# Output projection with weight rows outermost, 512 columns in four PSUM banks, for four of six token groups

## The chip, the cores and the metric

The kernel runs on one core of one Trainium2 chip. The metric is the device time of one execution in microseconds (us), lower is better. The engines work from queues of their own: TensorE (PE in the rows; PEld is its weight load), VectorE (DVE), ScalarE (ACT), GpSimd (POOL) and SyncE (SP, which here only issues DMAs). They meet through semaphores.

## The reference, cut to what matters

Two token groups, p (1024 tokens) and s (512 tokens), go through the same two layers. Each layer projects the normed input, runs three attention or convolution branches of 1280 columns together, gates them, and ends with the step that is changed here:

```python
y = jnp.concatenate([y1, y2, ym], axis=-1)          # (tokens, 1280)
x = x + (y * jax.nn.silu(z)) @ w_out[l]             # w_out[l]: (1280, 1024)
```

Layer 0 feeds layer 1, whose first step is an RMS norm over the rows of x.

## The kernel before

**Output projection.** `out_proj` handles 512 tokens at a time, so there are six token groups: p layer 0 halves 0 and 1, s layer 0, p layer 1 halves 0 and 1, s layer 1. Every fp32 operand is split into a high and a low part, and each product is three matmuls: high by high, high by low, low by high (L322, L323, L324 in `mm_a`). The outer loop takes 256 of the 1024 output columns at a time (`ci`, four of them). For each, `load_w` fetches five weight tiles of 256 KB (two rows of 128 contraction channels by 256 columns) and splits them. Then come four tiles of 128 tokens, and inside each the ten contraction rows k: 4 x 4 x 10 x 3 = 480 matmuls of 256 columns per group. Two token tiles share one PSUM bank of tag "d" (two banks in all); when both are complete, VectorE adds the residual at L935 and the sum goes to DRAM, as 8 evictions and 8 stores per group.

**Buffers.** `whi`, `wlo` (split weights) have 7 buffers, `wraw` 3, `bw` (residual rows among others) 5, `act` (gated branch outputs `ahi`, `alo`) 16. PSUM has two banks each of tags s, t and d, and one each of x and o. The banks of tag "t" hold the transposed probabilities `pT`, the small sums `ss` and the gate rows `rbT` of attention.

**Order of the work.** `STEPS` lists the phases. A planner then orders each engine's queue at compile time from this list and its own estimate of times. Attention phases (`ax`, `diff`, `mem_attn`) are marked urgent, so projections fill TensorE in between. `in_order` adds one more rule: the tiles of one ring (tag and stream) are first written in the order of the list. On the chip each queue runs in the order that was laid down.

**Around the groups.** Each layer 0 group of p is followed by a norm (`norm_steps`): load rows of x1, square, scale, transpose on TensorE (`hT`), store. It is doled out by `between` in the matmul loops. The list ends with attention of s layer 1, "diff s 2", "diff s 3", "mem s 1", and then the three last output projections: p layer 1 half 0, p layer 1 half 1, s layer 1. The last needs the results of "mem s 1" (`ym`).

Of the kernel before, what the change touches and what calls it, by code (L numbers as in the profile page):

```python
# [9 lines left out]
F32 = mybir.dt.float32  # L10
BF16 = mybir.dt.bfloat16
F32R = mybir.dt.float32r
ACTF = mybir.ActivationFunctionType
ALU = mybir.AluOpType
# [23 lines left out]
STEPS = [  # L38
# [11 lines left out]
]  # L50
BUF_TABLE = {
# [30 lines left out]
def trunk_kernel(ctx: ExitStack, tc: tile.TileContext, a: dict, dbg=None):  # L82
    nc = tc.nc
# [93 lines left out]
    S = {}  # L177
# [36 lines left out]
        return g  # L214

    @first
    def load_w(src, pairs):
        hi, lo = [], []
        for kp in pairs:
            lo_ = ring(sb, [128, 2, 256], F32R, "wlo", "wlo")  # L220
            h = ring(sb, [128, 2, 256], F32R, "whi", "whi")
            raw = ring(sb, [128, 2, 256], F32, "wraw", "wraw")
            dma(out=raw, in_=src[kp].rearrange("p (k n) -> p k n", k=2))
            split(h, lo_, raw, nc.vector if kp % 2 == 0 else nc.gpsimd)
            hi.append(h)
            lo.append(lo_)
        return hi, lo

    def rstd(out, ss, mul, add):
# [84 lines left out]
    def mm_a(out, hs, sl, w, mid=None):  # L314

        whi, wlo = w
        n = 2 * len(hs)
        for k in range(n):
            hi, lo = hs[k // 2]
            h, l_ = hi[:, k % 2, sl], lo[:, k % 2, sl]  # L320
            wh, wl = whi[k // 2][:, k % 2, :], wlo[k // 2][:, k % 2, :]
            nc.tensor.matmul(out=out, lhsT=h, rhs=wh, start=(k == 0), stop=False)  # L322
            nc.tensor.matmul(out=out, lhsT=h, rhs=wl, start=False, stop=False)  # L323
            nc.tensor.matmul(out=out, lhsT=l_, rhs=wh, start=False, stop=(k == n - 1))  # L324
            if mid and k == n // 4:
                mid()

    def mm_b(out, hs, w, csl, mid=None):

        whi, wlo = w  # L330
        n = 2 * len(hs)
        for k in range(n):
            hi, lo = hs[k // 2]
            h, l_ = hi[:, k % 2, :], lo[:, k % 2, :]
            wh, wl = whi[k // 2][:, k % 2, csl], wlo[k // 2][:, k % 2, csl]
            nc.tensor.matmul(out=out, lhsT=wh, rhs=h, start=(k == 0), stop=False)  # L336
            nc.tensor.matmul(out=out, lhsT=wh, rhs=l_, start=False, stop=False)  # L337
            nc.tensor.matmul(out=out, lhsT=wl, rhs=h, start=False, stop=(k == n - 1))  # L338
            if mid and k == n // 4:
                mid()  # L340
# [577 lines left out]
    def out_proj(g, l, hf, ys, ahead=None):  # L918
        T = GROUPS[g]
        src = a[f"x_{g}"] if l == 0 else S[g, "x1"]  # L920
        dst = S[g, "x1"] if l == 0 else a[f"out_{g}"]
        for ci in range(4):
            if ahead and ci == 3:
                ahead()
            w = load_w(a["w_out"][l, ci], Y_ORDER[g, l])
            for tp in range(2):
                ps = ring(psum, [128, 2, 256], F32, "d", "po")
                for t in range(2):
                    tt = 2 * tp + t
                    mm_a(ps[:, t, :], ys, slice(tt * 128, (tt + 1) * 128), w, lambda: between(0))  # L930
                rows = slice(hf * 512 + tp * 256, hf * 512 + (tp + 1) * 256)
                cols = slice(ci * 256, (ci + 1) * 256)
                xr = bw("xr").rearrange("p (t n) -> p t n", t=2)
                dma(out=xr, in_=src[rows, cols].rearrange("(t p) n -> p t n", p=128))
                nc.vector.tensor_tensor(out=xr, in0=ps, in1=xr, op=ALU.add)  # L935
                dma(out=dst[rows, cols].rearrange("(t p) n -> p t n", p=128), in_=xr)


    nxt = {}
# [27 lines left out]
    YS, YM = {}, {}  # L967
# [6 lines left out]
    def step(op, g, *x):  # L974
        if op == "in":
            l = int(x[0])
# [32 lines left out]
        elif op == "loady":  # L1009
            settle()  # L1010
            l, hf = int(x[0]), int(x[1])
            part = slice(int(x[2]), int(x[3])) if len(x) > 2 else slice(0, 5)
            YS.setdefault((g, l, hf), []).extend(load_y(g, l, hf, part))
        elif op == "memkv":
            mem_kv(1, H["m"])
        elif op == "out":
            l, hf = int(x[0]), int(x[1])
            out_proj(g, l, hf, YS[g, l, hf] + ([YM[l]] if g == "s" else []))
        elif op == "settle":
            settle()  # L1020

# [9 lines left out]
def host_arrays(inputs):  # L1031
# [29 lines left out]
    def pieces(w, idx):  # L1061
# [8 lines left out]
    out["mem_s"] = f["mem_sample"][0]  # L1070
    out["w_in"] = np.stack([np.stack([pieces(f["w_in"][l], cols(l, *c)) for c in CHUNKS[l]]) for l in range(2)])
    out["w_out"] = np.stack(
        [np.stack([pieces(f["w_out"][l], np.arange(256 * c, 256 * c + 256)) for c in range(4)]) for l in range(2)])
    out["w_mem_kv"] = np.stack(
        [np.stack([pieces(f["w_mem_kv"][l], np.arange(256 * c, 256 * c + 256)) for c in range(2)]) for l in range(2)])
    out["conv_w"] = f["conv_w"][0].reshape(3, 4, 128).transpose(2, 1, 0)
# [58 lines left out]
```

## Time and profile before

| | us |
|---|---|
| median of 3 runs | 2108.88 (2107.57 to 2109.26) |
| the profiled execution | 2099.39 |
| span of the profiled execution | 2097.6 |
| TensorE busy | 2040.2 |
| VectorE busy | 1552.4 |
| ScalarE busy | 1115.9 |
| GpSimd busy | 969.9 |

Busy times are unions of an engine's instructions. Matmuls overlap in the pipeline, so the time from one start to the next, not a matmul's own duration, is what one costs.

### The profile page before, as it was taken

What the parts mean: (1) busy time and instruction counts of PE and PEld (TensorE: products, weight loads), DVE (VectorE), ACT (ScalarE), POOL (GpSimd) and SP (SyncE); (2) the same over time, 40 slices, a digit from 0 to 9 for tenths busy, and PEclk for the clock granted to TensorE, in tenths of its full rate; (3) what the DMA queues carried; (4) which work ended last, traced back from release to release, by engine and by line L of the source; (5) the groups of instructions that cost most, each with busy time, mean ns of one, the idle gap of its engine ahead of it and who ended that gap; (6) DMA issues with size and microseconds to landing.
All of it is one profiled execution on the core that took longest, in us unless ns stands there. A gap on an engine that the chain in (4) does not pass through costs nothing.

```text
span 2097.6 us, 40483 instructions
## 1 busy us (share of the span) xinstructions
PE 2040.2 (97%) x14056; PEld 1885.0 (90%) x14056; DVE 1552.4 (74%) x3340; ACT 1115.9 (53%) x2634; POOL 969.9 (46%) x994
## 2 busy tenths in 40 slices
PE   6999999999999999999999899999998999999999
PEld 6999888889999899998999888888997898989999
DVE  8779877645446697887869998878879877876642
ACT  5545433453334466665667655566566665654531
POOL 6753422342224564645636564343363785833411
PEclk9999999999999999999999999999999999999999
DMA  7786733336777732354255756466576567577753
GB/s 236 206 241 197 228 106 91 118 101 217 238 236 224 209 93 82 104 154 128 82 151 154 226 164 178 151 199 213 169 218 199 160 191 193 157 235 225 233 159 106
DMA packets 323420, 365.79 MB, mean 174 GB/s; under 512 B 28048, under 2 KB 229520, under 8 KB 323216
## 3 DMA queue, kind: packets, MB, share of 16 engines
q1 hardware_dynamic: 323216, 363.21, 58.1%
q8 instruction: 111, 1.82, 0.4%
q14 instruction: 93, 0.76, 0.1%
HBM read 263.48 MB, written 99.61 MB: 173 GB/s over the span
## 4 chain that ended last, share of the span: by engine, by line
PE 75%; DMA 7%; DVE 7%; issue 3%; POOL 2%; ACT 1%; SPq 1%; DVEq 0%; POOLq 0%; ACTq 0%
PE pb L338 8%; PE pb L336 8%; PE pb L337 8%; PE pa L323 5%; PE pa L324 5%; PE pa L322 5%; PE po L322 4%; PE po L323 4%; PE po L324 4%; PE s L596 4%; PE s L597 4%; PE o L754 3%; PE pT L750 3%; PE o L685 1%; PE pT L683 1%
## 5 line engine op out<-in xcount | busy, mean ns | idle before, releaser
L200 POOL TENSOR_TENSOR wlo<-wraw,whi 128x512 fp32r<-128x512 f32 x182 | 249.0, 1370 | 329.1 <-ACT whi L199 309.9
L695 ACT ACTIVATE e<-s,nm 128x512 f32<-128x512 f32 (+1 forms) x416 | 265.1, 640 | 221.2 <-DVE nm L693 167.4
L199 ACT CAST whi<-wraw 128x512 fp32r<-128x512 f32 x388 | 236.9, 622 | 238.8 <-PE po L324 84.6
L604 DVE TENSOR_TENSOR ptlo<-pT,pthi 128x512 fp32r<-128x512 f32 x352 | 237.3, 683 | 41.6 <-ACT pthi L603 40.0
L693 DVE TENSOR_REDUCE nm<-s 128x1 f32<-128x512 f32 (+1 forms) x368 | 249.0, 682 | 25.7 <-PE s L597 24.4
L603 ACT CAST pthi<-pT 128x512 fp32r<-128x512 f32 x352 | 199.1, 588 | 114.6 <-PE pT L683 56.6
L322 PE MATMUL po<-whi,ahi 128*128 128x256 f32 x896 | 254.0, 284 | 0.4 <-DVE xr L935 0.4
L324 PE MATMUL po<-whi,alo 128*128 128x256 f32 x896 | 253.1, 284 | 1.3 <-DVE alo L200 1.3
L323 PE MATMUL po<-wlo,ahi 128*128 128x256 f32 x896 | 254.2, 284 | 0.0
L200 DVE TENSOR_TENSOR wlo<-wraw,whi 128x512 fp32r<-128x512 f32 x206 | 170.8, 830 | 95.3 <-ACT whi L199 92.5
L236 POOL TENSOR_TENSOR rs<-ss,mhalf 128x8 f32<-128x8 f32 (+2 forms) x108 | 141.1, 1307 | 174.4 <-DVE ss L232 125.2
L322 PE MATMUL pa<-whi,ahi 128*128 128x256 f32 x768 | 220.2, 287 | 0.5 <-ACT raw L394 0.4
L324 PE MATMUL pa<-whi,alo 128*128 128x256 f32 x768 | 219.2, 286 | 0.5 <-DVE alo L200 0.5
L323 PE MATMUL pa<-wlo,ahi 128*128 128x256 f32 x768 | 219.2, 285 | 0.0
L596 PE MATMUL s<-k,qhh 128*128 128x512 f32 (+2 forms) x512 | 190.1, 376 | 10.5 <-ACT e L695 9.6
L597 PE MATMUL s<-k,qll 128*128 128x512 f32 (+2 forms) x512 | 182.9, 363 | 2.8 <-DMA qll<-st_p1mq 1.6
L324 PEld LDWEIGHTS po<-whi,alo 128*128 128x128 f32 x896 | 171.0, 191 | 3.2 <-DVE alo L200 1.7
L322 PEld LDWEIGHTS po<-whi,ahi 128*128 128x128 f32 x896 | 171.1, 191 | 1.9 <-DVE xr L935 0.6
L323 PEld LDWEIGHTS po<-wlo,ahi 128*128 128x128 f32 x896 | 171.1, 191 | 1.2
L336 PE MATMUL pb<-h,whi 128*128 128x512 f32 x432 | 170.9, 396 | 0.0
L338 PE MATMUL pb<-h,wlo 128*128 128x512 f32 x432 | 170.7, 395 | 0.0
L337 PE MATMUL pb<-h,whi 128*128 128x512 f32 x432 | 170.6, 395 | 0.0
(170 smaller groups left out, 6022.7 us busy)
## 6 DMA issues: line engine op xcount, KB each, us to landing
wraw<-in_w_in_dram SPq DMA_DIRECT2D x252, 256.0 KB, 3.3
wraw<-in_w_out_dram SPq DMA_DIRECT2D x120, 256.0 KB, 3.2
alo<-y_p SPq DMA_DIRECT2D x20, 512.0 KB, 5.3
zg_p<-z SPq DMA_DIRECT2D x32, 256.0 KB, 2.7
v<-dv_p SPq DMA_DIRECT2D x16, 512.0 KB, 5.5
k<-st_p1dk SPq DMA_DIRECT2D x16, 512.0 KB, 4.3
zg<-zg_p SPq DMA_DIRECT2D x48, 128.0 KB, 3.0
y_p<-yo SPq DMA_DIRECT2D x48, 128.0 KB, 2.4
```

The source lines that it names most:

```text
L200: lo_eng.tensor_tensor(out=out_lo, in0=src, in1=f32(out_hi), op=ALU.subtract)
L322: nc.tensor.matmul(out=out, lhsT=h, rhs=wh, start=(k == 0), stop=False)
L323: nc.tensor.matmul(out=out, lhsT=h, rhs=wl, start=False, stop=False)
L324: nc.tensor.matmul(out=out, lhsT=l_, rhs=wh, start=False, stop=(k == n - 1))
L336: nc.tensor.matmul(out=out, lhsT=wh, rhs=h, start=(k == 0), stop=False)
L337: nc.tensor.matmul(out=out, lhsT=wh, rhs=l_, start=False, stop=False)
L338: nc.tensor.matmul(out=out, lhsT=wl, rhs=h, start=False, stop=(k == n - 1))
L596: nc.tensor.matmul(out=out, lhsT=q2[0], rhs=k, start=True, stop=False)
L597: nc.tensor.matmul(out=out, lhsT=q2[1], rhs=k, start=False, stop=True)
L604: nc.vector.tensor_tensor(out=lo, in0=ps, in1=f32(hi), op=ALU.subtract)
L693: nc.vector.tensor_reduce(out=nm, in_=s, axis=AXL.X, op=ALU.max, negate=True)
L695: nc.scalar.activation(out=e[:, j, :], in_=s[:, j, :], func=ACTF.Exp, bias=nm[:, j:j + 1], accum_out=su[:, j:j + 1],)
```

## The change

Four of the six groups (both halves of p layer 0, half 1 of p layer 1, s layer 1) use a new function, `out_proj_k`. It takes 512 columns at a time, with the weight rows k as the outer loop and four token tiles inside, each in a PSUM bank of its own: two of tag "d" and two of tag "t". That is 2 x 10 x 4 x 3 = 240 matmuls of 512 columns per group. The weights in DRAM are laid out anew (before the launch) as rows of 512 columns; the two groups that keep `out_proj` read their 256 columns out of these rows in pieces of 1 KB. The list of phases keeps its order.

```diff
-    "loady p 0 1", "out p 0 0", "norm p 0", "out p 0 1", "norm p 1", "load m", "load p 1 01", "memkv m",
+    "loady p 0 1", "outk p 0 0", "norm p 0", "outk p 0 1", "norm p 1", "load m", "load p 1 01", "memkv m",
...
-    "loady p 1 1", "out p 1 0", "loady s 1 0 0 4", "out p 1 1", "out s 1 0",
+    "loady p 1 1", "out p 1 0", "loady s 1 0 0 4", "outk p 1 1", "outk s 1 0",
...
-    def load_w(src, pairs):
+    def load_w(src, ks, wide=False):
+        for k in ks:
...
+            raw = ring(sb, [128, 512], F32, "wraw", "wraw")
+            dma(out=raw if len(src.shape) == 3 else raw.rearrange("p (i n) -> p i n", i=2), in_=src[k])
+            split(h, l_, raw, nc.vector if k % 2 == 0 else nc.gpsimd)
...
-            w = load_w(a["w_out"][l, ci], Y_ORDER[g, l])
+            w = load_w(
+                a["w_out"][l, ci // 2][:, :, ci % 2 * 256:ci % 2 * 256 + 256].rearrange("(k i) p n -> k p i n", i=2), Y_ORDER[g, l]
+            )
...
+    def out_proj_k(g, l, hf, ys):
+        src = a[f"x_{g}"] if l == 0 else S[g, "x1"]
+        dst = S[g, "x1"] if l == 0 else a[f"out_{g}"]
+        order = [2 * kp + i for kp in Y_ORDER[g, l] for i in range(2)]
+        for ci in range(2):
+            cols = slice(ci * 512, (ci + 1) * 512)
+            rows = [slice(hf * 512 + t * 128, hf * 512 + (t + 1) * 128) for t in range(4)]
+            ps = [ring(psum, [128, 512], F32, "d", "pk") for _ in range(2)]
+            ps += [ring(psum, [128, 512], F32, "t", "pk", "A") for _ in range(2)]
+            xr = []
+            for n, k in enumerate(order):
+                (wh,), (wl,) = load_w(a["w_out"][l, ci], [k], True)
+                hi, lo = ys[n // 2]
+                for t in range(4):
+                    sl = slice(t * 128, (t + 1) * 128)
+                    h, l_ = hi[:, n % 2, sl], lo[:, n % 2, sl]
+                    nc.tensor.matmul(out=ps[t], lhsT=h, rhs=wh, start=(n == 0), stop=False)
+                    nc.tensor.matmul(out=ps[t], lhsT=h, rhs=wl, start=False, stop=False)
+                    nc.tensor.matmul(out=ps[t], lhsT=l_, rhs=wh, start=False, stop=(n == 9))
+                if n < 9:
+                    between(0)
+                if n >= 5 and n < 9:
+                    x = bw("xr")
+                    dma(out=x, in_=src[rows[n - 5], cols])
+                    xr.append(x)
+            for t in range(4):
+                nc.vector.tensor_tensor(out=xr[t], in0=ps[t], in1=xr[t], op=ALU.add)
+                dma(out=dst[rows[t], cols], in_=xr[t])
```

## Rows read from the trace of the kernel before

**Rows 1.** The page, parts 1 and 4: busy time, and the chain that ended last.

```profile
PE 2040.2 (97%) x14056; PEld 1885.0 (90%) x14056; DVE 1552.4 (74%) x3340; ACT 1115.9 (53%) x2634; POOL 969.9 (46%) x994
...
PE 75%; DMA 7%; DVE 7%; issue 3%; POOL 2%; ACT 1%; SPq 1%; DVEq 0%; POOLq 0%; ACTq 0%
```

**Rows 2.** Busy time by stretch: PE, PEld, DVE, ACT, POOL; granted clock, DMA share, GB/s.

```profile
503.00:551.00 48.00, 48.00 (x403) 48.00 (x402) 12.95 (x20) 11.39 (x19) 8.00 (x6) 1.00 0.58 182
551.00:562.00 11.00, 9.01 (x72) 8.28 (x70) 8.74 (x12) 7.20 (x13) 4.01 (x4) 1.00 0.88 294
...
630.00:640.00 10.00, 8.26 (x68) 8.03 (x69) 8.71 (x17) 7.26 (x14) 4.70 (x5) 1.00 0.98 333
...
1965.00:2013.00 48.00, 47.23 (x385) 46.19 (x384) 30.34 (x51) 25.41 (x57) 15.92 (x18) 1.00 0.65 212
2036.00:2094.00 58.00, 57.77 (x482) 57.50 (x480) 14.98 (x21) 10.25 (x17) 7.98 (x7) 1.00 0.39 125
```

**Rows 3.** Timeline of TensorE: start, length, instruction; first and last of three runs.

```profile
324.26 0.40 PE L338 MATMUL pb<-h,wlo 128*128 128x512 f32 x1
...
327.25 0.39 PE L336 MATMUL pb<-h,whi 128*128 128x512 f32 x1
...
479.77 0.39 PE L336 MATMUL pb<-h,whi 128*128 128x512 f32 x1
...
493.14 0.39 PE L338 MATMUL pb<-h,wlo 128*128 128x512 f32 x1
...
494.80 0.28 PE L322 MATMUL po<-whi,ahi 128*128 128x256 f32 x1
...
501.52 0.28 PE L324 MATMUL po<-whi,alo 128*128 128x256 f32 x1
```

**Rows 4.** Timeline of VectorE, evictions: last of p layer 1 halves, last of all.

```profile
1968.55 0.69 DVE L935 TENSOR_TENSOR xr<-po,xr 128x512 f32<-128x512 f32 x1
...
2036.55 0.68 DVE L935 TENSOR_TENSOR xr<-po,xr 128x512 f32<-128x512 f32 x1
...
2093.80 0.69 DVE L935 TENSOR_TENSOR xr<-po,xr 128x512 f32<-128x512 f32 x1 [6.48 <-PE po L324]
```

**Rows 5.** Timeline of TensorE, end of attention.

```profile
1984.46 0.51 PE L829 MATMUL ss<-ones,zg 128*128 128x2 f32 x4
...
1989.22 0.27 PE L847 MATMUL rbT<-ident_r,yo 128*128 128x128 f32 x1
...
2007.32 0.60 PE L898 MATMUL pT<-ident_r,e 128*128 128x128 f32 x4
...
2012.51 0.40 PE L900 MATMUL o<-ptlo,v 128*128 128x512 f32 x1
```

**Rows 6.** Timeline of the other engines, single steps of attention's chain.

```profile
1985.79 1.01 POOL L836 TENSOR_TENSOR s<-s,mhalf 128x4 f32<-128x4 f32 x1 [0.70 <-DVE s L833]
1986.83 0.48 DVE L838 TENSOR_SCALAR yo<-ident_r,s 128x128 f32<-128x128 f32 x2 [0.44 <-POOL s L836]
...
1993.07 0.59 ACT L603 CAST pthi<-pT 128x512 fp32r<-128x512 f32 x1 [2.41 <-PE pT L898]
...
1993.69 0.69 DVE L604 TENSOR_TENSOR ptlo<-pT,pthi 128x512 fp32r<-128x512 f32 x1 [2.30 <-ACT pthi L603]
```

**Rows 7.** Timeline of the SP queue, residual stream after half 1 of p layer 0.

```profile
611.94 0.80 SPq L119 DMA_DIRECT2D x<-x_p  x2
...
617.25 0.38 SPq L119 DMA_DIRECT2D x_p<-xr  x1
```

**Rows 8.** DMA issues by line: count, KB each, median us to landing.

```profile
wraw<-in_w_out_dram SPq DMA_DIRECT2D x120, 256.0 KB, 3.2
...
xr<-in_x_p_dram SPq DMA_DIRECT2D x16, 256.0 KB, 5.7
```

**Rows 9.** Busy time by stretch around the one dip of the clock.

```profile
38.00:40.00 2.00, 0.00 (x0) 0.00 (x0) 2.00 (x5) 1.93 (x4) 1.59 (x2) 0.98 0.39 113
40.00:41.00 1.00, 0.41 (x2) 0.41 (x3) 1.00 (x4) 0.54 (x3) 0.00 (x0) 0.50 0.90 217
```

More of the change, by code (lines that the diff above doesn't have):

```diff
@@ L216, in load_w @@
     @first
-    def load_w(src, pairs):
+    def load_w(src, ks, wide=False):
         hi, lo = [], []
[L219 to L226, printed above, removed]
+        for k in ks:
+            l_ = ring(sb, [128, 512], F32R, "wlo", "wlo")
+            h = ring(sb, [128, 512], F32R, "whi", "whi")
+            raw = ring(sb, [128, 512], F32, "wraw", "wraw")
+            dma(out=raw if len(src.shape) == 3 else raw.rearrange("p (i n) -> p i n", i=2), in_=src[k])
+            split(h, l_, raw, nc.vector if k % 2 == 0 else nc.gpsimd)
+            for i in range(1 if wide else 2):
+                sl = slice(0, 512) if wide else slice(256 * i, 256 * i + 256)
+                hi.append(h[:, sl])
+                lo.append(l_[:, sl])
         return hi, lo
@@ L320, in mm_a @@
             h, l_ = hi[:, k % 2, sl], lo[:, k % 2, sl]
-            wh, wl = whi[k // 2][:, k % 2, :], wlo[k // 2][:, k % 2, :]
+            wh, wl = whi[k], wlo[k]
             nc.tensor.matmul(out=out, lhsT=h, rhs=wh, start=(k == 0), stop=False)
@@ L334, in mm_b @@
             h, l_ = hi[:, k % 2, :], lo[:, k % 2, :]
-            wh, wl = whi[k // 2][:, k % 2, csl], wlo[k // 2][:, k % 2, csl]
+            wh, wl = whi[k][:, csl], wlo[k][:, csl]
             nc.tensor.matmul(out=out, lhsT=wh, rhs=h, start=(k == 0), stop=False)
@@ L1015, in step @@
             mem_kv(1, H["m"])
-        elif op == "out":
+        elif op in ("out", "outk"):
             l, hf = int(x[0]), int(x[1])
-            out_proj(g, l, hf, YS[g, l, hf] + ([YM[l]] if g == "s" else []))
+            (out_proj_k if op == "outk" else out_proj)(g, l, hf, YS[g, l, hf] + ([YM[l]] if g == "s" else []))
         elif op == "settle":
@@ L1072, in host_arrays @@
     out["w_out"] = np.stack(
-        [np.stack([pieces(f["w_out"][l], np.arange(256 * c, 256 * c + 256)) for c in range(4)]) for l in range(2)])
+        [f["w_out"][l].reshape(10, 128, 2, 512).transpose(2, 0, 1, 3) for l in range(2)])
     out["w_mem_kv"] = np.stack(
```

## The prediction

> **What bounds the kernel now.** I read the page first, for the bound: TensorE is busy 2040.2 of 2097.6 us and three quarters of the chain that ended last lies on it [rows 1]. Then the busy times by stretch, over the phases that the edit touches: inside an output projection without attention TensorE is busy 48.00 of 48.00 us at a granted clock of 1.00 (the level of 2.4 GHz), with DMA at 0.58 and VectorE at about a quarter [rows 2]. So in these phases time is the number of matmuls times the distance from one start to the next, and that distance is what to look for in TensorE's timeline. Last, the end of the program, where three output projections serve as filler for the last attention: there the question is what TensorE has to do when a filler may no longer run. The same view shows it busy 47.23 of 48.00 us from 1965 to 2013 [rows 2].
>
> **The matmuls.** In `out_proj` 57 matmuls of 256 columns start between 494.80 and 501.52, so 6.72/56 = 0.1200 us each [rows 3]. 512 columns with the same weight load occur in the input projection (`pb`): 60 starts from 479.77 to 493.14 give 13.37/59 = 0.2266 us; with attention mixed in nearby, 14 starts from 324.26 to 327.25 give 0.230 us [rows 3]. A group costs 480 x 0.1200 = 57.6 us now, and the gap between the last evictions of the last two groups, 2093.80 - 2036.55 = 57.25 us, confirms it [rows 4]. Changed, it costs 240 x 0.2266 = 54.4 us, or 55.2 at 0.230. Saved are 3.2 us a group (2.4 at worst), 12.8 us for four (9.6 at worst). I take 12.8: three of the four groups run without attention.
>
> The Trainium skill (TensorE: Matmul & The Clock Gate, Back-to-back issue gap) puts the isolated distance at columns/2.4 + 2.5 ns, hence 109.2 ns for 256 and 215.8 ns for 512 columns. By it two small matmuls exceed one large by 2.6 ns, and the edit would give 4 x 240 x 2.6 ns = 2.5 us, an estimate. The trace disagrees: 0.1200 and 0.2266 us, a difference of 13.4 ns, and these rows decide.
>
> **The same work in other pieces.** Weight tiles (20 of 256 KB a group), splits, residual loads, evictions and stores (8 each a group) keep number and size; the edit of `load_w` into slices adds no instruction, and the layout is made before the launch. In p layer 0 two of 20 subtractions a group move from VectorE to GpSimd, which is busy 8.00 of 48 us there [rows 2]. A weight row now lasts 12 x 0.2266 = 2.7 us on TensorE against 3.2 us to landing [rows 8], with three loads in flight: covered. The two groups that keep `out_proj` read 1 KB pieces. Residual rows with such pieces take up to 5.7 us to landing where a weight tile takes 3.2 [rows 8]; seven split buffers hide the 2.5 us, and with that cover gone it would cost them once at each of two groups, 5 us. I take 0.
>
> **Start of half 1 of p layer 0.** From 551 to 562 TensorE is idle 11.00 - 9.01 = 1.99 us [rows 2], because `out_proj` wants all five branch pairs within its first 30 matmuls (3.6 us) while they are still being split. The new loop wants the last pair after eight of ten rows, 22 us in. Gain 0 to 2.0; I take 1.5, since the transposes of the norm stay.
>
> **Bank turns.** Each bank is complete 9 matmuls (2.0 us) before its successor is wanted, and its eviction takes 0.69 us [rows 4]. VectorE has 1.35 us to come to it, at a load of a quarter. Seven turns at 0 to 1.35 us: 0 to 9, I take 0.5.
>
> **The end.** The last eviction and its store stay, but three stores of 256 KB go out within the 2 us before. Cost 0 to 2 us (three times the 0.69 us eviction); I take 0.4.
>
> **End of half 1 of p layer 0.** Now the first two loads of x1 rows for the norm go out at 611.94, 5.3 us ahead of the last store at 617.25 [rows 7]. In the new loop all four token tiles finish within 2 us of the end, so these loads come up to 5.3 us later. Behind them on the SP queue stand the loads for the next input projection; ahead of it TensorE has only the memory projection, 192 x 0.12 = 23 us, and it is already idle 1.74 us in 630 to 640, with DMA at 0.98 [rows 2]. Against that, `out_proj` holds all ten `act` tiles until its last token tile, while the new loop frees a pair after every two rows of its second half, the first 22 us ahead of the end. The next loads spread out and that jam eases. Bounds -1.7 to +5.3; I take 0.
>
> **The last attention, the term that decides.** The banks of tag "t" form one ordered ring. `out_proj_k` for half 1 of p layer 1 stands after "mem s 1" in the list, so its third and fourth banks may be written only after the last transposes of "mem s 1". Before, that group was filler during this attention: its predecessor's last eviction is at 1968.55, its own at 2036.55, and attention's last matmul is at 2012.51 [rows 4, 5]. From there it ran alone for (2036.5 - 2012.9)/0.12 = 197 matmuls, so 283 of its 480, or 34.0 us, had filled gaps. Changed, only banks one and two can start, for as many weight rows as `whi` has buffers: 7 x 6 x 0.2266 = 9.5 us. If attention keeps its pace, TensorE misses 34.0 - 9.5 = 24.5 us: the upper bound. The lower is 0, if attention closes up entirely.
>
> It should close up in large part, since most of its time was queueing behind filler. From the end of the `o` before it, the square, the sums `ss` (0.51), scale, power (1.01), fill (0.48) and `rbT` need about 3.5 us with hand-overs; the rows show 1989.22 - 1984.46 = 4.8 us from `ss` to `rbT` alone [rows 5, 6]. Then "mem s 1" has four heads of two transpose groups. One group is 0.60 on TensorE, 0.59 on ScalarE, 0.69 on VectorE [rows 5, 6], 2.2 us to the first `o` with hand-overs; after that a head is paced by VectorE, four operations of 0.69 us, 2.75 us. That is 2.2 + 11.0 = 13.2 us where the rows show 2012.9 - 1989.3 = 23.6 [rows 5]; banks three and four join 2.9 us before its end. So 3.5 + 13.2 - 2.9 = 13.8 us run without filler. Attention's own matmuls in them are 8 groups of transposes at 0.45 us from start to start, 12 `o` of 0.23 us and 0.6 us of small ones, 7.0 us. Idle: 6.8 us. I take 7, nearer the low bound, because the steps measured one by one are short.
>
> The clock fell once, to 0.50 (1.2 GHz), after TensorE had idled all of 38 to 40 us [rows 9]. The gaps expected here are shorter and broken by matmuls; if it fell, each us at that level would give back half of itself.
>
> **Sum.** -12.8 - 1.5 + 0.5 + 0.4 + 0 + 7.0 = -6.4 us, so 2099.4 becomes 2093.0 for a profiled execution. That one lies 9.5 us under the median of the runs, 2108.88; carried over, the forecast is **2102.5 us**. A difference under 0.2% (4.2 us) is about what a measurement cannot tell from none.
>
> **Rivals.**
> A, the forecast: idle 4 to 12 us in the last attention, 2099 to 2107. Chance 0.45, two thirds of it beyond 4.2 us.
> B, the last attention closes up wholly, or the planner lays the partial rows where the gaps are: term 0, so -13.4, 2095.5. For it: VectorE is busy only 30.34 and ScalarE 25.41 of 48 us there [rows 2]. Chance 0.2.
> C, the other side: attention keeps its pace without filler, 24.5 us idle, -13.4 + 24.5 = +11.1, 2120. It decides from 13.4 us of idle time on. For it: the queues were laid down by the planner's estimates, and other casts stand between the steps in ScalarE's queue. Against it: each step's own time. Chance 0.15.
> D, the change saves next to nothing per column, two small matmuls costing as much as a large one (0.240): the 12.8 vanish, +6.4, 2115. The operands do change places, weights now move and activations are loaded; but three runs of starts speak against it. By the formula of the Trainium skill's page named above, 2.5 instead of 12.8 us, it would be 2112.8. Chance 0.05.
> E, the norm after half 1 of p layer 0 comes late by its 5.3 us: -1.1, 2107.8. Chance 0.1.
> F, the planner lays out attention elsewhere differently, by more than 5 us either way. Chance 0.05.
>
> Faster by over 0.2%: 0.30 of A, B and half of F, 0.53. Within: 0.14 of A and E, 0.24. Slower: C, D and half of F, 0.23. Range: from B with the 2 us of the start and a little of the norm (2092) up to D (2115); most of C and the ends of F stay out, about 2 in 10. The forecast's own range is 2099 to 2107.
>
> **What would show it.** Right: `pk` matmuls 0.227 us apart, 54 us a group; no idle time at the start of half 1 of p layer 0; TensorE idle some 7 us in the gaps of "mem s 1", with `pk` in banks one and two only before its last transposes. Wrong: a distance near 0.24; idle time over 13 us before the last `pT`; or waits of `hT` on late x1 rows after p layer 0. A planner that shifts other phases would make it wrong with every step right.

## The result, and the profile after

The changed kernel took 2124.83 us in the median of 4 runs (2120.36 to 2126.11) against 2108.39 us for the kernel before: ratio 1.0079, 95% interval 1.0063 to 1.0096, slower by 0.8%. The forecast was 2102.5 us with a range of 2092 to 2115 and a gain as the likeliest sign; the time lies above the range, and the sign is the other one. A second series of the same program (told below) gave a ratio of 1.0040 (1.0024 to 1.0056): slower again, by about half as much. I give effects as ratios to the kernel before of the same series; 0.1% is 2.1 us.

The page of the changed kernel, its part 1 (busy time of each engine, share of the span, instructions), stands beside [rows 1].

```profile
span 2123.9 us, 38525 instructions
...
PE 2043.7 (96%) x13096; PEld 1841.0 (87%) x13096; DVE 1547.0 (73%) x3332; ACT 1113.0 (52%) x2634; POOL 984.0 (46%) x1002
```

TensorE has 960 matmuls less and is busy 3.5 us longer, where 12.8 us less were to come, and its idle time went from 57.4 us to 80.2 us. A longer busy time with fewer matmuls means that some ran slower. So there are two things to look for, waits and the clock. The profiled execution of the kernel before is a fast one, which makes these differences look large: its 2099.39 us lie below all of the 141 executions of that kernel in the experiments (lowest 2100.08).

First the matmuls themselves. The timeline of TensorE, first and last of 90 starts in the first changed group:

```profile
504.82 0.39 PE L964 MATMUL pk<-whi,alo 128*128 128x512 f32 x1
...
524.99 0.39 PE L963 MATMUL pk<-wlo,ahi 128*128 128x512 f32 x1
```

20.17/89 = 0.2266 us, to the last digit the distance that the input projection showed [rows 3]. The timeline of VectorE in the last two groups (each row is four evictions, of one half of a group):

```profile
2063.53 2.73 DVE L972 TENSOR_TENSOR xr<-pk,xr 128x512 f32<-128x512 f32 x4 [2.01 <-PE pk L964]
...
2118.20 2.78 DVE L972 TENSOR_TENSOR xr<-pk,xr 128x512 f32<-128x512 f32 x4 [15.94 <-PE pk L964]
```

The last group lasts from 2063.53 to 2118.20, 54.67 us, where the last group before took 57.25 [rows 4]. That part of the sum came true, with 2.6 us here in place of 3.2. Now the waits of TensorE (waiting line, releaser, us in total, times, longest), from 550 to 680:

```profile
PE hT L270 <- DVE ht L281: 6.2, 4, 2.4
PE pm L326 <- DVE xr L972: 1.7, 1, 1.7
...
PE hT L270 <- DVE x L263: 1.3, 1, 1.3
```

and from 1900 to 2110:

```profile
PE o L822 <- ACT pthi L607: 6.1, 2, 4.3
PE rbT L851 <- DVE yo L842: 2.3, 2, 1.8
PE ss L833 <- ACT zg L827: 0.9, 2, 0.5
```

Two places, then: the norms (`hT`) around the two halves of p layer 0, and the last attention. Busy times by stretch (PE, PEld, DVE, ACT, POOL, then granted clock, DMA share, GB/s) show that the clock fell at both:

```profile
551.00:562.00 11.00, 11.00 (x51) 9.06 (x50) 5.88 (x9) 3.53 (x7) 1.84 (x3) 1.00 0.95 326
578.00:581.00 3.00, 0.95 (x5) 0.45 (x3) 2.79 (x3) 1.31 (x3) 1.75 (x2) 1.00 0.96 333
581.00:584.00 3.00, 2.67 (x9) 2.08 (x10) 3.00 (x6) 0.00 (x0) 0.00 (x0) 0.65 0.67 193
...
632.00:636.00 4.00, 2.04 (x8) 1.23 (x7) 2.48 (x4) 0.62 (x1) 1.00 (x2) 0.50 1.05 291
...
1980.00:2000.00 20.00, 16.61 (x100) 14.08 (x98) 12.24 (x23) 10.37 (x26) 9.95 (x12) 1.00 0.76 256
2000.00:2020.00 20.00, 14.20 (x63) 11.03 (x64) 11.12 (x21) 10.43 (x24) 3.57 (x6) 0.74 0.14 47
```

551 to 562 has no idle time any more, as forecast. But further on, at 578 to 581, TensorE waits 2.35 us for the norm's step `ht` on VectorE. From 1980 to 2020 it is busy 30.81 of 40 us, and a granted clock of 0.74 over 20 us is 10.4 us at the lower of the two levels (0.50, 1.2 GHz). That costs at most half of it, 5.2 us, and less as far as TensorE is idle in them.

### The profile page after: what moved, and what is told of

It is laid out like the page before. It is cut to its first block, busy times and chain, and to the rows that moved or that the text cites. A ratio compares the mean times of both kernels' runs of the same rounds, so it can differ in the third digit from the quotient of the medians.

```text
span 2123.9 us, 38525 instructions
## 1 busy us (share of the span) xinstructions
PE 2043.7 (96%) x13096; PEld 1841.0 (87%) x13096; DVE 1547.0 (73%) x3332; ACT 1113.0 (52%) x2634; POOL 984.0 (46%) x1002
## 5 line engine op out<-in xcount | busy, mean ns | idle before, releaser
L200 POOL TENSOR_TENSOR wlo<-wraw,whi 128x512 fp32r<-128x512 f32 x190 | 257.4, 1356 | 339.2 <-ACT whi L199 306.5
L699 ACT ACTIVATE e<-s,nm 128x512 f32<-128x512 f32 (+1 forms) x416 | 264.6, 640 | 236.4 <-DVE nm L697 167.3
L200 DVE TENSOR_TENSOR wlo<-wraw,whi 128x512 fp32r<-128x512 f32 x198 | 157.4, 796 | 108.8 <-ACT whi L199 108.2
L600 PE MATMUL s<-k,qhh 128*128 128x512 f32 (+2 forms) x512 | 192.3, 381 | 14.8 <-ACT e L699 12.5
L341 PE MATMUL pb<-h,whi 128*128 128x512 f32 x432 | 170.4, 394 | 0.0
L326 PE MATMUL pa<-whi,h 128*128 128x256 f32 x576 | 165.5, 287 | 1.8 <-ACT h L295 1.0
L328 PE MATMUL pa<-whi,h 128*128 128x256 f32 x576 | 165.6, 288 | 0.4 <-DVE h L296 0.4
L327 PE MATMUL pa<-wlo,h 128*128 128x256 f32 x576 | 164.8, 286 | 0.3 <-POOL wlo L200 0.3
L326 PEld LDWEIGHTS pa<-whi,ahi 128*128 128x128 f32 x768 | 146.7, 191 | 4.9 <-ACT ahi L199 0.9
L328 PEld LDWEIGHTS pa<-whi,alo 128*128 128x128 f32 x768 | 146.8, 191 | 4.1 <-DVE alo L200 1.0
L327 PEld LDWEIGHTS pa<-wlo,ahi 128*128 128x128 f32 x768 | 146.7, 191 | 3.9
```

What stands on the lines that cost most here:

```text
L200: lo_eng.tensor_tensor(out=out_lo, in0=src, in1=f32(out_hi), op=ALU.subtract)
L600: nc.tensor.matmul(out=out, lhsT=q2[0], rhs=k, start=True, stop=False)
L699: nc.scalar.activation(out=e[:, j, :], in_=s[:, j, :], func=ACTF.Exp, bias=nm[:, j:j + 1], accum_out=su[:, j:j + 1],)
```

## The experiments

**Theory 1**, formed on these rows: the change loses in two separate places. In p layer 0 all x1 rows of a group are complete only at its end, so the norm's loads hold up the SP and VectorE queues into the next group. In the last attention filler is missing, as forecast, and the clock falls on top. **Rivals:** the new layout's 1 KB pieces cost; the new loop costs wherever it stands; the planner's other order of the queues does it.

**One part alone.** Five kernels have the new layout, and none or one of the four groups in the new loop. Each differs from the changed kernel in the list of phases only; half 1 of p layer 1 alone, for instance:

```diff
-    "loady p 0 1", "outk p 0 0", "norm p 0", "outk p 0 1", "norm p 1", "load m", "load p 1 01", "memkv m",
+    "loady p 0 1", "out p 0 0", "norm p 0", "out p 0 1", "norm p 1", "load m", "load p 1 01", "memkv m",
...
-    "loady p 1 1", "out p 1 0", "loady s 1 0 0 4", "outk p 1 1", "outk s 1 0",
+    "loady p 1 1", "out p 1 0", "loady s 1 0 0 4", "outk p 1 1", "out s 1 0",
```

The layout alone: 

> No group uses the new loop; only the layout of the weights in DRAM is new, so all six groups read 1 KB pieces. Theory 1 (the loss sits at two places, the norm after half 1 of p layer 0 and the last attention): same as before, within 3 us. Rival (the 1 KB pieces cost, two groups of six in the change): 5 us or more slower here, with six groups of six. Rival 2 (any edit makes the planner lay the queues anew, and that is the loss): off by 5 us or more in either direction.

Half 0 of p layer 0: 

> Only half 0 of p layer 0 uses the new loop. Theory 1: 3.2 us faster than before from the matmuls (0.2266 against 2 x 0.1200 us), up to 5 with the start, since half 1 still covers the norm of half 0. Rival 2 (planner): anything between 10 us slower and 5 faster, with the loss spread over the phases behind.

Half 1 of p layer 0: 

> Only half 1 of p layer 0 uses the new loop. Theory 1: the norm of half 1 starts late, TensorE idles and its clock halves around the memory projection; 8 to 12 us slower than before by the end of that stage. Rival (the loss after p layer 0 comes from half 0): 3 us faster.

Half 1 of p layer 1: 

> Only half 1 of p layer 1 uses the new loop. Theory 1: its third and fourth banks wait for the last transposes of the last attention, 9 to 14 us idle with a dip of the clock, 3.2 us saved on matmuls: 6 to 11 us slower. Rival (the loss at the end came down from earlier phases): 3 us faster.

s layer 1: 

> Only the last group, s layer 1, uses the new loop. Nothing runs beside it and nothing but the last store comes after. Theory: the 3.2 us of the matmuls are kept, against at most 1 us at the end: 2 to 4 us faster than the run with the layout alone (2105.3). Rival (the new loop gains nothing per column): same as the layout alone.

| new loop in | median us | ratio (95%) | over layout only | forecast for the group |
|---|---|---|---|---|
| none (layout only) | 2105.31 | 0.9982 (0.9969 to 0.9994) | | 0 |
| p layer 0, half 0 | 2108.49 | 0.9998 (0.9985 to 1.0011) | +3.4 us | -3.2 - 1.5 |
| p layer 0, half 1 | 2107.48 | 0.9995 (0.9983 to 1.0008) | +2.7 us | -3.2 + 0 |
| p layer 1, half 1 | 2116.74 | 1.0037 (1.0024 to 1.0051) | +11.6 us | -3.2 + 7.0 |
| s layer 1 | 2104.52 | 0.9984 (0.9969 to 0.9998) | +0.4 us | -3.2 + 0.4 |

A difference of two such ratios is uncertain by about 0.2%, 4 us. The layout costs nothing (it lies 0.2% under the kernel before, less than two series of one kernel differed by in the end). Three groups of four come out above their forecast by 6 to 8 us, which is more than the uncertainty; the sign of s layer 1 is not settled by this row. The expectations for both halves of p layer 0 were missed as well: 3 to 5 us faster than before for half 0, 8 to 12 us slower for half 1, and both came out level with it. That for half 1 of p layer 1, 6 to 11 us slower, held.

What half 0's trace shows: the SP queue, first with half 0 changed, then with the layout alone. `x<-x_p` are the norm's loads of x1 rows, `x_p<-xr` the stores of them.

```profile
551.45 0.86 SPq L119 DMA_DIRECT2D x_p<-xr  x2
553.18 4.86 SPq L119 DMA_DIRECT2D x<-x_p  x2
```

```profile
548.60 0.81 SPq L119 DMA_DIRECT2D x<-x_p  x2
553.92 0.37 SPq L119 DMA_DIRECT2D x_p<-xr  x1
```

Two loads hold the queue for 4.86 us, right behind the last of the four stores, where two took 0.81 us ahead of the last store. VectorE (same kernel, its timeline) then waits for those rows, and the eviction of the next group's first bank stands behind that wait:

```profile
558.22 0.15 DVE L236 TENSOR_SCALAR ss<-ss 128x1 f32<-128x1 f32 x1 [3.79 <-ACT sqx L260]
562.24 0.15 DVE L236 TENSOR_SCALAR ss<-ss 128x1 f32<-128x1 f32 x1 [2.44 <-ACT sqx L260]
...
564.63 0.68 DVE L941 TENSOR_TENSOR xr<-po,xr 128x512 f32<-128x512 f32 x1
```

TensorE's waits from 550 to 590, half 0 changed:

```profile
PE po L326 <- DVE xr L941: 4.6, 2, 3.1
```

**Three attempts at a single cause.** In all three the theory's forecast was missed and the rival's time came true. The norm's steps after half 0 delayed by five empty ones, so that they come behind the first eviction:

```diff
-                BG.extend(norm_steps(rows_of(S["p", "x1"], hf), put_dram(S["p", 1, "h"], 512 * hf, g1)))
+                BG.extend([lambda: None] * (5 if hf == 0 else 0) + norm_steps(rows_of(S["p", "x1"], hf), put_dram(S["p", 1, "h"], 512 * hf, g1)))
```

> As p00, but the steps of the norm of half 0 are doled out two calls of between (some 7 us) later. Theory: in p00 the norm's loads and VectorE operations stood at the head of their queues before the rows of x1 had landed, and held up residual loads and evictions of half 1; later, they find their rows: TensorE's waits on VectorE in half 1 go, and the 3.2 us show, 3 to 7 us faster than p00. Rival (p00 lost by the planner's new order elsewhere): same as p00 within 2 us.

Measured: 2106.05 us, 0.9995 (0.9984 to 1.0005). The wait on the eviction is gone from the trace (TensorE waits 0.8 us in all from 550 to 590), but the time differs from that of half 0 undelayed by 0.03%, no more than noise. On the SP queue the two loads still take 4.67 us. The wait behind the eviction is thus not the price, or not the whole of it.

Half 1 of p layer 0 with its last 512 columns by token pairs, each pair with a weight load of its own, so that half of the x1 rows are complete earlier:

```diff
+    PARTS = {("p", 0, 1): [[((0, 1, 2, 3), "dt")], [((0, 1), "d"), ((2, 3), "t")]]}
...
+            for ts, tag in PARTS.get((g, l, hf), WHOLE)[ci]:
```

> As p01, but the last 512 columns are taken for two token tiles and then for the other two, with the weight rows loaded twice, so that half of the x1 rows are complete 13 us before the end. Theory (late x1 rows make the norm late): TensorE's idle time and the dip of the clock around the memory projection shrink, 3 to 6 us faster than p01. Rival (the loss is the planner's, or the dip comes from DMA traffic): same or slower than p01, as ten more weight rows are loaded.

Measured: 2113.26 us, 1.0027 (1.0015 to 1.004), worse by 0.3% than without the pairs. In its trace `hT` waits 6.6 us in all from 560 to 700 (5.5 of them for `x`), where half 1 without pairs has 5.1, and the DMA share from 562 to 616 is 0.89 against 0.84. The ten loads of 256 KB that it adds may be what costs; no run holds them apart from the earlier rows. Half 1 of p layer 1 in the two d banks alone, two token tiles at a time, weights loaded twice:

```diff
+    PARTS = {("p", 1, 1): [[((0, 1), "d"), ((2, 3), "d")]] * 2}
```

> As p11, but two token tiles at a time in the two banks of tag d alone, so that the new loop never waits for the banks of attention; the weight rows are loaded twice (20 more loads). Theory (the ordered ring of tag t takes the filler from the last attention): the idle time and the dip of the clock at the end go, 8 to 11 us faster than p11, so 1 to 3 us faster than before. Rival (the new loop is slow there for its loads or evictions): as slow as p11 or slower, with twice the loads.

Measured: 2121.01 us, 1.0066 (1.0051 to 1.008), worse than with the t banks. Here TensorE waits 4.1 us at one place in "mem s 1" and 2.4 us for evictions of the new loop. It speaks neither for nor against the t banks: with the order of the ring it also changed the loads and the turns.

**Half and half.** The next edit adds no load and no bank. A group does two of its four column blocks as before and the other 512 columns the new way: in p layer 0 the new way first, so that x1 rows become complete token pair by token pair at the end; in p layer 1 the old way first, so that filler stands ready.

```diff
+            elif op == "outfk":
+                out_proj(g, l, hf, ys, None, (0, 1))
+                out_proj_k(g, l, hf, ys, (1,))
+            else:
+                out_proj_k(g, l, hf, ys, (0,))
+                out_proj(g, l, hf, ys, None, (2, 3))
```

Half 1 of p layer 1, old way first: 

> Only half 1 of p layer 1 differs from the layout-only kernel (median 2105.3 us, 0.9982 of before): its first 512 columns go token tile by token tile in the two d banks as before (240 matmuls of 256 columns, 28.8 us, free to fill the last attention), its last 512 columns go the new way. Theory that the last attention lacks filler because banks three and four wait for its transposes: 28.8 us plus the 9.5 us that two banks may start are more than the 34.0 us of gaps filled before, so no idle time and no fall of the clock is added, and one half saves 1.6 us: 2103.7 us, ratio 0.997 to 0.999; TensorE busy over 46.5 of 48 us in the stretch of the last attention. Rival, that the new loop itself costs in the tail (its loads, its late residual rows, its evictions four at a time), whatever fills the gaps: about half of the 9 to 11 us that the full change of this group cost, 2109 to 2111, ratio over 1.001.

Half 0 of p layer 0, new way first: 

> Only half 0 of p layer 0 differs from the layout-only kernel: its first 512 columns go the new way, its last 512 columns as before, so x1 rows of the first two token tiles are complete 7.2 us ahead of the group's end again and their stores are spread. Theory that the full change of this group gave its 3.2 us back because all x1 rows came in the last 2 us and the norm's loads stood before other loads on the SP queue: the loss is gone, 1.6 us are saved, 2103.7 us, ratio 0.9965 to 0.999, no wait over 2.5 us on VectorE between 550 and 565, and no wait of TensorE on an eviction over 1 us in 564 to 584. Rival, that what is lost is that four residual rows and evictions of the new loop crowd the start of half 1 (they are still there at the middle of the group, not at its end) or that the planner's other order does it: 2106 to 2109, ratio 0.9995 or more.

The first of these together with s layer 1 wholly new: 

> Half 1 of p layer 1 mixed (first 512 columns as before, last 512 the new way), and s layer 1 wholly the new way; both halves of p layer 0 as before. If the effects of the groups add and the filler theory holds: layout only 2105.3, minus 1.6, minus the 0.8 that s layer 1 alone measured (3.2 by the matmuls' distance): 2100.5 to 2103, ratio 0.9965 to 0.998. If the new loop itself costs in the tail: 2108 or more.

All four groups so repaired: 

> Both halves of p layer 0 with the first 512 columns the new way and the last 512 as before, half 1 of p layer 1 the other way round, s layer 1 wholly the new way: the change without the three things that by the theory gave its saving back (late x1 rows after both halves of p layer 0, no filler for the last attention). Matmuls saved: 3 x 1.6 + 3.2 = 8.0 us. Theory: 2105.3 - 8.0 to 2105.3 - 5.6 (s layer 1 at its measured 0.8): 2097 to 2100, ratio 0.995 to 0.997. Rival, that other costs come with the new loop wherever it stands: 2104 to 2112, ratio 0.9985 or more. Rival, a planner's reordering of the stretch between the layers of 3 to 12 us either way, as seen in the traces with half 1 of p layer 0 changed: it would show in offsets between 700 and 1600 us, not in the four groups.

| kernel | median us | ratio (95%) |
|---|---|---|
| p layer 1 half 1, old way first | 2107.65 | 1.0000 (0.9987 to 1.0013) |
| p layer 0 half 0, new way first | 2103.00 | 0.9981 (0.9966 to 0.9996) |
| p layer 1 half 1 mixed, s layer 1 new | 2103.16 | 0.9978 (0.9962 to 0.9994) |
| all four repaired | 2099.73 | 0.9959 (0.9944 to 0.9973) |

The mix takes 0.37% (7.8 us) off the price of half 1 of p layer 1. That is a recovery, though not the gain that was expected (0.997 to 0.999): 1.0000 is above the layout alone, within the uncertainty. For half 0 of p layer 0 the time is in the range of the theory, but one of its signs is not: TensorE should have waited no more than 1 us for an eviction from 564 to 584, and waits 1.9 us. s layer 1 now shows its gain: 0.9978 against 1.0000, 4.6 us with the same uncertainty of 4, by the matmuls 3.2. The kernel with all four repaired is at the forecast of theory 1 and faster than both kernels, so the new loop does not cost wherever it stands. Where the filler is back, the last attention is full (1980 to 2020; half 1 of p layer 1 wholly new, then mixed, one row from each kernel):

```profile
1980.00:2020.00 40.00, 33.16 (x152) 26.46 (x151) 23.38 (x38) 18.15 (x38) 11.82 (x14) 0.87 0.28 92
```

```profile
1980.00:2020.00 40.00, 40.00 (x311) 38.56 (x310) 26.85 (x46) 21.81 (x47) 15.61 (x17) 1.00 0.62 191
```

6.84 us of idle time on one side, none on the other, and a clock of 0.87 (10.4 of 40 us at the lower level) against 1.00.

**Late rows, or fewer new matmuls?** The mix in half 0 also halved the new matmuls. So the same mix the other way round (`outfk p 0 0`), which keeps the rows late; and, in the changed kernel, each of the two repairs by itself.

Half 0, new way last: 

> Half 0 of p layer 0 alone, mixed the other way round: first 512 columns as before, last 512 the new way. As many new matmuls as in the mixed run before (1.6 us saved), but all x1 rows are complete only in the last 2 us again. Theory of the late rows: the gain is gone, 2106 to 2109 us, ratio 0.9995 or more, TensorE waits on an eviction in 564 to 584 again by 2 us or more. Rival, that the halved number of new matmuls and evictions was what recovered it: 2102 to 2104.5, ratio 0.9985 or less.

Changed kernel, tail repaired: 

> The changed kernel (2124.8 us), with half 1 of p layer 1 alone mixed (first 512 columns as before, last 512 the new way). Theory that the last attention's lack of filler costs 9 to 13 us of the change: 2112 to 2116 us, ratio 1.002 to 1.004, and the stretch of the last attention at TensorE over 46 of 48 us and a clock of 1.00. Rival, that most of the loss comes in p layer 0 once both halves are changed: 2118 or more.

Changed kernel, p layer 0 repaired: 

> The changed kernel (2124.8 us), with both halves of p layer 0 mixed (first 512 columns the new way, last 512 as before) and the tail left as the change has it. Theory that late x1 rows cost the two halves what the single changes showed (3.2 and 2.2 us over layout only, and 1.6 each that the mixed order saves): 2124.8 - 8.6 = 2116 us, 2114 to 2119, ratio 1.0035 to 1.0055. If the effects add, the two recoveries of this call sum to the 25 us between the changed kernel and the one with all four repaired. Rival, that the tail is nearly the whole of it: 2120 or more.

Half 0 with the new way last took 2106.40 us, 0.9997 (0.9981 to 1.0014), as slow as wholly new (0.9998), and the same rows come back: SP queue and TensorE's waits of this kernel,

```profile
556.40 0.85 SPq L119 DMA_DIRECT2D x_p<-xr  x2
558.29 5.01 SPq L119 DMA_DIRECT2D x<-x_p  x2
```

```profile
PE po L326 <- DVE xr L941: 4.5, 2, 2.6
```

against new way first:

```profile
548.05 0.81 SPq L119 DMA_DIRECT2D x<-x_p  x2
553.47 0.37 SPq L119 DMA_DIRECT2D x_p<-xr  x1
```

```profile
PE po L326 <- DVE xr L941: 1.9, 1, 1.9
PE hT L270 <- DVE ht L281: 1.7, 1, 1.7
```

Same number of new matmuls, 0.16% apart (3.4 us, less than the uncertainty of 0.2%). The queues differ as the theory of the late rows says. The waits differ less: 3.6 us in all from 550 to 590 with the rows early, 5.3 us with them late, 1.3 us with the layout alone. The changed kernel with the tail repaired took 2106.97 us, 0.9992 (0.9974 to 1.0009); with p layer 0 repaired 2108.97 us, 1.0002 (0.9984 to 1.0019). Both recovered more than expected from 2124.8 us: 17.9 and 15.9 us, together 33.7, while the kernel with both repairs lies only 25.1 us lower. Either the two losses make each other larger, or 2124.8 was high. So the changed kernel was run again, unaltered, and with it the repaired one without its mix in half 1 of p layer 1:

> The changed kernel once more, unaltered. If the two losses add: 2099.7 us with all repaired, plus 7.2 for p layer 0 (2106.97 - 2099.73) plus 9.2 for the tail (2108.97 - 2099.73), 2116.2 us, 2113 to 2119, ratio 1.003 to 1.0055. If they make each other larger: 2121 to 2127 as first measured, ratio 1.0065 or more.

> The kernel with all four groups repaired (2099.7 us), with half 1 of p layer 1 wholly as before. By the distance of the matmuls the mixed half saves 1.6 us there, so without it 2101.3 us; by the single run of that half (2.3 us over layout only) it costs, so without it 2097.4 us. The two differ by 3.9 us, ratio 0.9968 against 0.995.

The changed kernel: 2114.44 us, 1.0040 (1.0024 to 1.0056). The two losses add. From the repaired kernel, 0.9959, p layer 0 costs 0.0033 (0.9992 - 0.9959, 7.0 us) and the tail 0.0043 (1.0002 - 0.9959, 9.1 us), 1.0035 in all. The last kernel took 2097.85 us, 0.9955 (0.9937 to 0.9972), so the mix in half 1 of p layer 1 brings nothing that can be told from none. The best version has the new loop in s layer 1 and for the first 512 columns of both halves of p layer 0, nowhere else; it is 0.45% faster than the kernel before.

**The same effects in the traces.** Two stretches begin and end at the same instructions in all 19 profiled executions, with the same work between but for the changed matmuls. The first goes from layer 0's last `o` matmul ahead of p's output projections to the first `s` matmul of layer 1's attention (`s` are attention's scores, `o` its results). It takes 232.3 to 242.1 us with both halves of p layer 0 as before (seven executions, median 236.3), 236.1 to 239.0 with both new (three), 240.1 and 240.5 with half 1 alone new, 226.0 to 229.2 with both mixed (three). One of each by busy times: both new (the changed kernel), as before (half 1 of p layer 1 alone new), both mixed (all four repaired).

```profile
472.86:711.83 238.97, 225.71 (x1269) 197.08 (x1267) 117.89 (x185) 86.91 (x159) 79.83 (x76) 0.96 0.70 220
```

```profile
476.85:711.29 234.44, 226.10 (x1750) 218.90 (x1748) 120.98 (x190) 87.18 (x160) 77.30 (x73) 0.99 0.72 226
```

```profile
475.41:704.58 229.17, 222.93 (x1509) 206.75 (x1508) 118.10 (x188) 87.20 (x160) 79.16 (x75) 0.99 0.73 231
```

By the matmuls both new should lie 6.4 us under the median and half 1 alone 3.2; they lie 0.2 under to 2.7 above it, and 4 above. All five executions with half 1 wholly new (one of them by token pairs) have TensorE idle 11.4 to 13.3 us here and a clock of 0.96. The other fourteen have 5.4 to 12.5 us and 0.98 to 1.00. In the rows, the changed kernel with 480 matmuls fewer keeps TensorE busy as long (225.7 us against 226.1). So about half of what is lost here is slower matmuls, and only the rest is waits. Both mixed have their 3.2 us and some more. Half 0 alone shows no loss here beyond the spread: 233.4 us wholly new, 236.4 new way first, 233.4 new way last, which is not the order of their medians.

The second stretch goes from the 60th last `o` matmul to the end: 170.4 to 175.1 us where the tail is as before (eight executions, median 172.85). s layer 1 new gives 169.69 and 170.99, half 1 of p layer 1 mixed 171.25, both 165.35 to 168.52 (three): 1.9 to 3.2, 1.6 and 4.3 to 7.5 us less, by the matmuls 3.2, 1.6 and 4.8. With half 1 of p layer 1 wholly new it takes 182.06 us (183.06 in the two d banks alone), and 177.67 to 179.46 us with s layer 1 new too (three): against the matmuls' saving 11 to 13 us lost. Between the two stretches, from the first `s` to the 100th last `o`, the four kernels with half 1 of p layer 0 wholly new take 1167.8 to 1172.1 us and the other fifteen 1162.8 to 1172.5, so a planner's other order costs nothing there that can be told.

## Why the prediction was wrong

**Right.** The distance (0.2266), the length of a group (54.67 us where the sum had 54.4), the start of half 1 of p layer 0 without idle time from 551 to 562, and, within the spread, the saving of 3.2 us where the group is the last (second stretch above). Rival D (512 columns as dear as two of 256) is out; its remark that the operands change places holds against the input projection only, for in `mm_a` too the activations are loaded and the weights move. By the Trainium skill (TensorE: Matmul & The Clock Gate, Back-to-back issue gap) the isolated distance for 512 columns would be 0.2158 us, and the saving by that formula 0.6 us a group, an estimate; the trace keeps 0.2266, and with it the 3.2 us. The repaired kernel realises it within the uncertainty: 4.8 us under the layout alone, by the matmuls 8.0, uncertain by 4. The bank turns were not all right: the sum has the seven inside the groups at 0.5, and the dearest is the one behind half 1 of p layer 0, where the memory projection (`pm`) waits for an eviction of the new loop, 1.7 us in the changed kernel, 1.9 in its second series, 2.7 with half 1 alone new.

**The step that failed first: the two terms for p layer 0, "Gain 0 to 2.0; I take 1.5" for the start of half 1 and "Bounds -1.7 to +5.3; I take 0" for its end.** The first asked when the new loop wants its activations, and of the norm that is doled out into the same stretch it counted the transposes alone, not that this norm needs half 0's x1 rows, which now come late. At the end of half 1 I had seen the same lateness, priced it at up to 5.3 us and taken 0; for half 0 the sum has no such term at all. In place of -4.7 us this group measured +3.4, half 1 +2.7 in place of -3.2. Shown is that the loss goes when both halves are mixed: 1.0040 becomes 1.0002, and with the tail repaired 0.9992 becomes 0.9959. That the late rows make it is likely and not shown. For it speaks the order of half 0's two mixes, 0.9981 with the rows early and 0.9997 with them late, which lies within the uncertainty; against it, that the delayed norm lost its waits and won no time. In the first stretch above the loss comes with half 1; half 0 alone, which carries the direct test, shows none there. Another difference was not tested: the new loop calls `between` 18 times a group, one weight row (2.7 us) apart, the old one 16 times, one token tile (3.6 us) apart, so the norm's steps come at other moments. Rival E had the late rows, at one of the two places and at a chance of 0.1. The hope set against them, "The next loads spread out and that jam eases", gained nothing that the first stretch shows. And no term for p layer 0 had the clock, 0.96 there in every execution with half 1 wholly new.

The profiled execution of before had a clock of 1.00 from 620 to 680. Of the six other executions with both halves of p layer 0 as before, four had 0.91 to 0.97 there. A stretch that most of them pass at a lower clock looked undisturbed in the one that the prediction rests on.

**The second: "The last attention", the ring right, the idle time right by some luck, the clock at nothing.** The banks in a ring order, the two banks that may start, 6.8 us of idle time: the kernel with this group alone changed shows 6.84. But 2.99 of them (2.65 before 1988.53 and 0.34 behind it) lie ahead of the stretch that was priced, which begins at "the end of the `o` before it"; that stretch itself has 3.85. The other 2.99 us are a wait that the sum did not have. In ScalarE's queue the cast `pthi` stands behind a cast `ahi` that waits for the activations of s layer 1, and by then the filler has run out, its last matmul ahead of the wait starting at 1985.48 (timelines of ScalarE and TensorE):

```profile
1986.40 1.14 ACT L199 CAST ahi<-alo 128x512 fp32r<-128x512 f32 x2 [2.48 <-DMA alo<-y_s]
...
1987.91 0.57 ACT L607 CAST pthi<-pT 128x512 fp32r<-128x512 f32 x1
```

```profile
1988.53 0.39 PE L822 MATMUL o<-pthi,v 128*128 128x256 f32 x1 [2.65 <-ACT pthi L607]
```

What was mis-sized is the clock, taken as 0 with "if it fell, each us at that level would give back half of itself". It fell, in the changed kernel after a wait of 4.33 us at the same place (timeline of TensorE):

```profile
2001.40 0.38 PE L822 MATMUL o<-pthi,v 128*128 128x256 f32 x1 [4.33 <-ACT pthi L607]
...
2008.90 1.11 PE L902 MATMUL pT<-ident_r,e 128*128 128x128 f32 x4 [0.58 <-DVE yo L852]
...
2010.24 0.63 PE L904 MATMUL o<-ptlo,v 128*128 128x512 f32 x1
```

One transpose group takes 1.11 us where it took 0.60, an `o` 0.63 where it took 0.40 [rows 5]. It hits the attention itself, which here sets the end. In the kernel with this group alone changed the lower level lasts from 1989.65 to 1999.89 (busy times):

```profile
1989.65:1999.89 10.24, 7.54 (x29) 5.99 (x29) 3.23 (x8) 2.92 (x8) 3.60 (x6) 0.50 0.20 64
```

TensorE is busy 7.54 us of these, so the clock costs at most 3.8 us. In the second stretch above this kernel lies 9.2 us over the median, 12.4 us with the 3.2 that it saves: 6.8 us more idle time and 5.6 us more busy time. So the term is 12.4 instead of 7; of the 5.4 us that were missing the clock is at most 3.8, and what the rest is stays open.

The argument that gaps "shorter and broken by matmuls" keep the clock up rests on a misreading: "The clock fell once" [rows 9]. In the same trace of the kernel before it fell three times, twice more after single waits of 1.27 and 2.31 us (timeline of TensorE, then busy times behind each):

```profile
1240.50 0.35 PE L597 MATMUL s<-k,qll 128*128 128x256 f32 x1 [1.27 <-DMA qll<-st_s0q]
...
1593.57 0.80 PE L596 MATMUL s<-k,qhh 128*128 128x512 f32 x1 [2.31 <-ACT e L695]
```

```profile
1241.00:1245.00 4.00, 4.00 (x23) 4.00 (x22) 3.41 (x8) 1.18 (x2) 1.45 (x2) 0.57 0.71 209
1593.00:1600.00 7.00, 6.43 (x24) 5.70 (x25) 6.90 (x16) 3.99 (x11) 1.97 (x2) 0.51 0.79 260
```

Both are waits between matmuls, of the kind that was taken as harmless, so this trace itself spoke against the zero.

**The sum with what was measured.** The four single effects and the layout: -3.8 + 3.4 + 2.7 + 11.6 + 0.4 = +14.3 us, between the two series of the changed kernel (+8.4 and +16.7). The agreement is loose, for each effect is uncertain by 4 us. Rival C named the side and in "other casts stand between the steps in ScalarE's queue" one of the waits, but not the mechanism: the attention did not keep its pace, it closed up as forecast.

**What stays open.** Why the first series lay 0.39% above the second, with the same program; their profiled executions differ by 11.2 us, in pieces. At 620 to 640 the clock was 0.74 in both, and the waits are the same ones, each somewhat shorter (`hT` on `ht` 4.4 us instead of 6.2, `o` on `pthi` 4.5 instead of 6.1). Why delaying the norm's steps removed the wait and not the time, and with it which part of the late norm costs p layer 0 its saving. And the planner's share inside the two stretches, where its order changes with the loop; no run isolates that.

## What to carry to other kernels

When a loop is turned so that all its results finish together, look first for the reader of the first result: here, with the norm's loads late, p layer 0 lost more than the larger matmuls saved, and a form that kept them early did not. A filler may be worth more as filler than as faster work: price what a bank's place in an ordered ring forbids, and then add the clock, after counting its falls over the whole trace and not at one place. Where only one end of a loop hurts, change the other half alone: in p layer 0 two halves of a group in different forms gave what neither form gave.

## What the runs showed of the hardware

The clock fell after waits that I had reckoned as harmless. In the changed kernel, timeline of TensorE around the wait in half 1 of p layer 0:

```profile
581.30 0.66 PE L270 MATMUL hT<-ident_r,x 128*128 128x128 f32 x4 [2.35 <-DVE ht L281]
581.99 0.77 PE L962 MATMUL pk<-whi,ahi 128*128 128x512 f32 x1
582.55 0.63 PE L963 MATMUL pk<-wlo,ahi 128*128 128x512 f32 x1
582.98 0.63 PE L964 MATMUL pk<-whi,alo 128*128 128x512 f32 x1
...
585.45 0.40 PE L964 MATMUL pk<-whi,alo 128*128 128x512 f32 x1
585.68 0.39 PE L962 MATMUL pk<-whi,ahi 128*128 128x512 f32 x1
```

After 2.35 us of waiting the matmuls start 0.43 us apart (582.98 - 582.55) instead of 0.2266, until 585.45. The eight that start from 581.99 on take 3.46 us instead of 1.81, so the wait cost some 1.6 us more than its own length. Not every such wait did it: with half 0 of p layer 0 changed, new way last, TensorE waits 2.58 us before 582.03 for an eviction, and the clock stays at its upper level (timeline, then busy times by stretch):

```profile
582.03 0.39 PE L326 MATMUL po<-whi,ahi 128*128 128x256 f32 x1 [2.58 <-DVE xr L941]
```

```profile
580.00:584.00 4.00, 1.97 (x16) 1.97 (x17) 2.55 (x4) 0.00 (x0) 0.59 (x2) 1.00 1.11 372
584.00:588.00 4.00, 4.00 (x36) 4.00 (x36) 0.96 (x2) 0.78 (x2) 0.00 (x0) 1.00 0.64 196
```

So a wait of 2 to 3 us may cost its own length or, as here, 1.7 times that, and these rows do not tell which it will be. The executions of one kernel spread along with the clock: 141 of the kernel before lie between 2100.08 and 2119.31 us (median 2107.45). The 42 with a mean granted clock above 0.9945 have a median of 2105.2 us, the 33 at or below 0.9925 one of 2110.2. So four runs are few for an effect of some tenths of a per cent: the two series of the changed kernel differed by 0.39%, more than either interval says.
